# A gate row applied to the finished projection on VectorE instead of to eight weight tiles on GpSimd

## The chip, the cores and the metric

The kernel runs on one core of one Trainium2 chip. The metric is the device time of one execution in microseconds (us), the median of several runs. The engines are named as in the profile: PE is TensorE, with its weight loads listed apart as PEld; DVE is VectorE; ACT is ScalarE; POOL is GpSimd; SP is SyncE, which here only issues transfers.

## The reference, cut to what matters

Two transformer blocks run on 256 tokens of width 1024. The change lies in the second block, where its mixer ends:

```python
sh1, sc1, gt1, sh2, sc2, gt2 = jnp.split(mod, N_MOD, axis=-1)
...
merged = jax.nn.sigmoid(gate_sb) * br_sb + jax.nn.sigmoid(gate_d) * br_d
x = x + gt1[:, None, :] * (merged @ w_out[layer])

h2 = modulate(rms_norm(x, g_ffn[layer]), sh2, sc2)
x = x + gt2[:, None, :] * peer_ffn(h2, w_pq[layer], peer_keys[layer], peer_u[layer], peer_v[layer])
```

`gt1` is one row of 1024 numbers. It scales the columns of the product, so it may be multiplied into the columns of `w_out` before the product, or into the product after it.

## The kernel before, in words

Everything is computed in float32. A product with a weight is made of three matmuls: a weight tile of 128 rows by 1024 columns is split into a high half `whi` (a rounded copy, made by ACT at L228) and a low half `wlo` (the tile minus its high half, a subtraction at L233, mostly on DVE, for a few tiles on POOL), and the activations likewise. Each weight tile is loaded whole (512 KB) into one of four buffers `raw`, in a ring: a load is issued by SP at L201 as soon as the low half of the tile four places ahead has been taken. `specs` lists the tiles in the order of use, with flags: "G" (multiply by the gate row first), "L" (keep the halves in the pool `late`, which has 7 buffers here), "P" (low half on POOL). `_split` handles one tile of that list: it issues the loads that have come due, and then splits the tile.

The stretch that the change touches comes in this order:

- The merge: for eight column tiles n, PE multiplies two attention outputs (`sbT`, `dT`) with the branch weights (L274: 12 matmuls and 6 of 256 columns for each n, so 18), DVE multiplies the two results with sigmoid gates (L1308, L1309, which read PSUM) and adds them (L1310), ACT copies the high half into `mT` (L1311), and DVE takes the low half (L1312).
- The projection with `w_out` of the second block, whose eight tiles are called out0 to out7 below: 12 matmuls of 512 columns for each tile. The first four tiles are done between the merges (`formA_acc`, L860), the last four in `acc_tail` (L875), which first finishes both halves of token tile 0 (24 matmuls), then the left and then the right half of token tile 1 (12 each). The results stand in four PSUM banks `acc`.
- The end (`epi`), for each token tile: add `acc` to the residual `x` (`add_x`, L1008), sums of squares on ACT (`sumsq`, L313), a reciprocal root in some ten small DVE instructions (`rsqrt`, L295 to L306), scaling (`scale_x`, L358 on ACT and L359 on DVE, giving `xn`), transposes on PE (L369), then scale and shift and the split into `h_hi` and `h_lo` (`norm_Tt`, L380 to L384).
- The next product, with `w_pq` (L1103, the first four of its 16 tiles called pq0 to pq3; their low halves are taken on POOL), then 12 more tiles at L274, the scores, a top-16 search on DVE, and two passes over 128 tiles each of `peer_u` (L1597) and `peer_v` (L1682). Beside these, rows for the first 96 tokens are gathered by POOL's queue into `ug`.

A scheduler sets the order of the instructions on each engine when the kernel is built, from its own estimate of times. Each engine works through its own list strictly in order, so an instruction that waits holds up all that stand behind it on that engine. Here are the functions that the change touches:

Of the kernel before, what the change touches and what calls it, by code (L numbers as in the profile page):

```python
# [9 lines left out]
F32 = mybir.dt.float32  # L10
# [6 lines left out]
OP = mybir.AluOpType  # L17
# [115 lines left out]
class Kernel:  # L133
# [4 lines left out]
    def specs(self):  # L138
        io = self.io
        sp = []  # L140

        def add(w, idx, flag="", late=0):
            idx = list(idx)
            for n, i in enumerate(idx):
                sp.append((w[i], flag + ("L" if n >= len(idx) - late else "")))
        add(io["w_in"], (0, 1, 2, 3, 12, 13, 14, 15, 4, 8, 5, 9, 6, 10, 7, 11))
        add(io["w_glu"], range(2), "R")
        add(io["w_out"], range(8), late=4)
        add(io["w_gu"], range(8), late=self.GL)
        nv = 0  # L150
        for j in range(4, NF):
            add(io["w_gu"], (2 * j, 2 * j + 1))
            add(io["w_down"], (j - 4,))
            for _ in range(self.JV[j]):
                add(io["w_in2"], (8 + nv,), "L")
                nv += 1
            if j >= NF - 4:
                add(io["w_down"], (j,), "L")
        add(io["w_in2"], range(8 + nv, 12))
        add(io["w_in2"], list(range(8)) + list(range(12, 46)))  # L160
        add(io["w_br"], range(6))
        for i in range(8):
            add(io["w_out2"], (i,), "G" + ("L" if i > 3 else ""))
        for i in range(4):
            add(io["w_pq"], (i,), "LP")
        add(io["w_pq"], range(4, 16))
        self.nwide = len(sp)
        add(io["peer_u"], range(128), "R")
        add(io["peer_v"], range(128), "R")
        return sp  # L170
# [39 lines left out]
    def _split(self, pin=lambda i: i):  # L210
        j = self.nsplit
        while self.ndma < len(self.wspec):
            early = self.depth > self.RAW and self.ndma - self.nwide < 24 + 2 * self.RB
            if self.ndma >= j + self.depth + (4 if early else 0):
                break
            self._dma()
        t = self.rawt.pop(j)
        flag = self.wspec[j][1]
        if "R" in flag:
            self.wt[j] = t  # L220
            self.nsplit += 1
            return
        if "G" in flag:
            self.nc.gpsimd.tensor_tensor(t, t, self.gt1, OP.mult)  # L224
        late = "L" in flag
        hi = (self.late if late else self.his).tile([128, 1024], F32R, name="whi")
        lo = (self.late if late else self.los).tile([128, 1024], F32R, name="wlo")
        i = self.nc.scalar.activation(hi, t, AF.Copy)  # L228
        pin(i)
        if self.fenced:  # L230
            self.behind(i, self.fence[0])
        e = self.nc.gpsimd if j in self.POOL_LO or "P" in flag else self.nc.vector
        i = e.tensor_tensor(lo, t, hi.bitcast(F32), OP.subtract)  # L233
        pin(i)
        if self.fenced:
            self.fenced -= 1
            if e is self.nc.vector:
                self.behind(i, self.fence[1])
        self.wt[j] = (hi, lo)
        self.nsplit += 1  # L240
# [761 lines left out]
                self.norm_Tt(H, xn, self.cols[:, C_GFFN:], None, self.h2[0], self.h2[1], tt)  # L1002
            self.acc_tail(acc, [(self.mixT, k) for k in range(4, 8)], False, epi, pre=self.PRE[0])

    def add_x(self, acc, tt, pin):
        for n in range(2):
            x = self.x[:, tt, 512 * n:512 * n + 512]
            i = self.nc.vector.tensor_tensor(x, x, acc[2 * tt + n], OP.add)  # L1008
            if tt and n < pin:
                self.tc.keep_in_program_order(i)  # L1010

# [210 lines left out]
    def block2(self):  # L1222
        nc, V, A, tc = self.nc, self.nc.vector, self.nc.scalar, self.tc
        with ExitStack() as st:
# [67 lines left out]
            with tc.tile_pool(name="mrg", bufs=2) as M, self.ps_pool("pa") as pa:  # L1292
                mT = [M.tile([128, 8, 256], F32R, name=f"mT{i}", bufs=1) for i in range(2)]
                acc = [self.bank(pa, f"acc{i}") for i in range(4)]
                for half in range(2):
                    wb = self.wget(2)
                    wa = [self.wget(1), self.wget(0)]
                    for q in range(4):
                        n = 4 * half + q
                        ps = self.psum()  # L1300
                        va = lambda w: (lambda k: w[:, (q % 2) * 512 + k * 128:(q % 2) * 512 + k * 128 + 128])
                        vb = lambda w: (lambda k: w[:, q * 256 + k * 128:q * 256 + k * 128 + 128])
                        self.mm3(ps[:, 0:256], va(wa[q // 2][0]), va(wa[q // 2][1]), lambda k: self.sbT[0][:, k],
                                 lambda k: self.sbT[1][:, k], 4)
                        self.mm3(ps[:, 256:512], vb(wb[0]), vb(wb[1]), lambda k: self.dT[0][:, k],
                                 lambda k: self.dT[1][:, k], 2)
                        a, b = [M.tile([128, 256], F32, name=f"mg{i}") for i in "ab"]
                        V.tensor_tensor(a, ps[:, 0:256], gates[:, n], OP.mult)  # L1308
                        V.tensor_tensor(b, ps[:, 256:512], gates[:, 8 + n], OP.mult)  # L1309
                        V.tensor_tensor(a, a, b, OP.add)  # L1310
                        A.activation(mT[0][:, n], a, AF.Copy)  # L1311
                        V.tensor_tensor(mT[1][:, n], a, mT[0][:, n].bitcast(F32), OP.subtract)  # L1312
                for n in range(4):
                    self.formA_acc(acc, mT, n, n == 0, False)
                self.h4 = self.bigT("h4")
                g, sh = self.mod_col(M, 4, "G2"), self.mod_col(M, 3, "sh2")

                def epi(tt):
                    self.add_x(acc, tt, self.XP[2])
                    yield  # L1320
                    r = self.rstd(M, self.x, tt, "n4")
                    if tt == 0:
                        self.r4 = self.cols[:, C_NCOL:C_NCOL + 1]
                        V.tensor_copy(self.r4, r)
                    xn = self.scale_x(M, self.x, r, tt)
                    yield
                    self.norm_Tt(M, xn, g, sh, self.h4[0], self.h4[1], tt)
                self.acc_tail(acc, [(mT, k) for k in range(4, 8)], False, epi, pre=self.PRE[2])


# [437 lines left out]
```

## Time and profile before

| what | value |
|---|---|
| median of 3 runs | 1325.82 us (1325.56 to 1333.4) |
| the profiled execution's own time | 1333.33 us |
| its span, first to last instruction | 1331.6 us |
| PE busy | 1246.1 us (94%) |
| DVE busy | 925.5 us (70%) |
| POOL busy | 464.3 us (35%) |
| POOL, L224, `raw` times `gt1` | 8 instructions, 21.2 us |

The busy shares are means over the whole span and hide that its stages have different limits. The rows further down come from one stretch of some 50 us, and each shows in square brackets how long the engine stood idle before the instruction, and what ended that wait. Two successive instructions of one engine overlap a little in these listings, so the distance from one start to the next is the better measure of what one costs in a sequence.

### The profile page before, as it was taken

What the parts mean: (1) busy time and instruction counts of PE and PEld (TensorE: products, weight loads), DVE (VectorE), ACT (ScalarE), POOL (GpSimd) and SP (SyncE); (2) the same over time, 40 slices, a digit from 0 to 9 for tenths busy, and PEclk for the clock granted to TensorE, in tenths of its full rate; (3) what the DMA queues carried; (4) which work ended last, traced back from release to release, by engine and by line L of the source; (5) the groups of instructions that cost most, each with busy time, mean ns of one, the idle gap of its engine ahead of it and who ended that gap; (6) DMA issues with size and microseconds to landing.
All of it is one profiled execution on the core that took longest, in us unless ns stands there. A gap on an engine that the chain in (4) does not pass through costs nothing.

```text
span 1331.6 us, 22565 instructions
## 1 busy us (share of the span) xinstructions
PE 1246.1 (94%) x8649; PEld 1162.7 (87%) x8650; DVE 925.5 (70%) x1806; ACT 447.2 (34%) x895; POOL 464.3 (35%) x408
## 2 busy tenths in 40 slices
PE   6798989999999999988899999999999999999994
PEld 5687869988979898986699999999999999888884
DVE  8995765899668887459789957677764444444455
ACT  5336655666556745634542212212110000000001
POOL 5931021555104745026300432222233333333331
PEclk9997889999999998998899999999999999999996
DMA  6322445989726645434758899999999999999993
GB/s 201 97 94 64 131 163 207 316 303 332 245 84 231 210 139 189 131 124 165 252 199 297 302 409 376 364 355 353 366 364 408 409 409 408 408 409 408 409 407 121
DMA packets 103116, 361.50 MB, mean 271 GB/s; under 512 B 15136, under 2 KB 15328, under 8 KB 102624
## 3 DMA queue, kind: packets, MB, share of 16 engines
q1 hardware_dynamic: 71904, 251.28, 51.9%
q0 software_dynamic: 30816, 108.26, 21.4%
q8 instruction: 68, 1.11, 0.3%
q10 hardware_dynamic: 288, 0.52, 0.1%
q14 instruction: 40, 0.33, 0.1%
HBM read 356.22 MB, written 2.12 MB: 269 GB/s over the span
## 4 chain that ended last, share of the span: by engine, by line
PE 44%; DMA 20%; DVE 18%; issue 9%; POOL 6%; ACT 2%; ACTq 0%; POOLq 0%; SPq 0%; DVEq 0%
PE m L1597 17%; DMA ug<-peer_v,slot 15%; PE m L274 14%; DVE wlo L233 4%; PE acc L860 3%; PE acc L1103 3%; DVE sacc L1518 2%; POOL ug L1501 2%; DMA adaw<-w_ada 2%; PE g L1553 1%; POOL adaacc L412 1%; PE acc L875 1%; PE pq L1103 1%; POOL adaacc L414 1%; DMA bias<-bias 1%
## 5 line engine op out<-in xcount | busy, mean ns | idle before, releaser
L1682 PE MATMUL acc<-act,raw 128*128 128x160 f32 x2048 | 296.4, 303 | 8.7 <-DMA raw<-peer_v 2.0
L1682 PEld LDWEIGHTS acc<-act,raw 128*128 128x128 f32 x2048 | 280.1, 190 | 24.9 <-DMA raw<-peer_v 23.3
L1597 PE MATMUL m<-hN,raw 128*128 128x160 f32 x2048 | 283.4, 300 | 2.6 <-ACT act L1607 2.6
L233 DVE TENSOR_TENSOR wlo<-raw,whi 128x1024 fp32r<-128x1024 f32 x150 | 237.7, 1595 | 67.4 <-ACT whi L228 64.7
L1597 PEld LDWEIGHTS m<-hN,raw 128*128 128x128 f32 x2048 | 278.9, 190 | 2.8 <-ACT act L1607 2.8
L228 ACT ACTIVATE whi<-raw 128x1024 fp32r<-128x1024 f32 x166 | 174.0, 1055 | 138.9 <-PE m L274 56.0
L1518 DVE SCALAR_TENSOR_TENSOR sacc<-ug,sw,sacc 128x1024 f32<-128x1024 f32 x94 | 120.8, 1285 | 122.2 <-DMA ug<-peer_v,slot 122.1
L1501 POOL DMA_INDIRECT ug<-u_rows,slot x96 | 97.5, 1015 | 212.8 <-DVE ug L1506 131.2
L1506 DVE SCALAR_TENSOR_TENSOR ug<-ug,hrow 128x1024 f32<-128x1024 f32 x96 | 117.2, 1222 | 45.8 <-DMA ug<-u_rows,slot 45.7
L1501 POOL DMA_INDIRECT ug<-peer_v,slot x96 | 91.5, 953 | 159.1 <-DVE sacc L1518 144.8
L274 PE MATMUL m<-h_hi,wlo 128*128 128x256 f32 x768 | 113.4, 288 | 7.4 <-DVE wlo L233 5.0
L274 PE MATMUL m<-h_hi,whi 128*128 128x256 f32 x768 | 117.1, 292 | 2.6 <-ACT h_hi L918 2.6
L274 PE MATMUL m<-h_lo,whi 128*128 128x256 f32 x768 | 117.0, 291 | 2.0 <-DVE h_lo L919 2.0
L274 PEld LDWEIGHTS m<-h_hi,whi 128*128 128x128 f32 x768 | 105.8, 197 | 7.1 <-ACT h_hi L918 3.5
L274 PEld LDWEIGHTS m<-h_hi,wlo 128*128 128x128 f32 x768 | 101.6, 193 | 9.8 <-DVE wlo L233 6.0
L274 PEld LDWEIGHTS m<-h_lo,whi 128*128 128x128 f32 x768 | 105.0, 197 | 3.3 <-DVE h_lo L919 2.4
L1689 ACT ACTIVATE fT<-acc,gt 128x160 f32<-128x160 f32 x4 | 1.3, 393 | 247.0 <-DVE fT L1691 247.0
L412 POOL TENSOR_TENSOR adaacc<-adaacc,adaw 128x1024 f32<-128x1024 f32 x24 | 66.5, 2770 | 49.3 <-ACT adaw L411 48.8
L1615 ACT ACTIVATE ut<-m 128x8 f32<-128x8 f32 (+19 forms) x84 | 20.2, 241 | 130.6 <-PE m L1597 130.5
L1618 DVE TENSOR_TENSOR act<-act,ut 128x8 f32<-128x8 f32 (+19 forms) x84 | 20.8, 247 | 52.2 <-ACT ut L1615 52.1
L233 POOL TENSOR_TENSOR wlo<-raw,whi 128x1024 fp32r<-128x1024 f32 x16 | 40.4, 2534 | 27.4 <-ACT whi L228 22.9
L224 POOL TENSOR_TENSOR raw<-raw,gt 128x1024 f32<-128x1024 f32 x8 | 21.2, 2664 | 56.9 <-DVE wlo L233 42.4
(522 smaller groups left out, 1774.4 us busy)
## 6 DMA issues: line engine op xcount, KB each, us to landing
raw<-peer_u SPq DMA_DIRECT2D x128, 512.0 KB, 6.6
raw<-peer_v SPq DMA_DIRECT2D x128, 512.0 KB, 20.1
raw<-w_in SPq DMA_DIRECT2D x62, 512.0 KB, 4.3
adaw<-w_ada SPq DMA_DIRECT2D x48, 512.0 KB, 5.3
raw<-w_gu SPq DMA_DIRECT2D x44, 512.0 KB, 4.9
raw<-w_down SPq DMA_DIRECT2D x22, 512.0 KB, 4.6
raw<-w_out SPq DMA_DIRECT2D x16, 512.0 KB, 3.4
raw<-w_pq SPq DMA_DIRECT2D x16, 512.0 KB, 5.0
```

Source lines behind the costliest of these rows:

```text
L224: self.nc.gpsimd.tensor_tensor(t, t, self.gt1, OP.mult)
L228: i = self.nc.scalar.activation(hi, t, AF.Copy)
L233: i = e.tensor_tensor(lo, t, hi.bitcast(F32), OP.subtract)
L274: self.nc.tensor.matmul(out, w(k), x(k), start=start and c == 0, stop=stop and c == last)
L412: G.tensor_tensor(accs[1], accs[1], w, OP.add)
L860: self.nc.tensor.matmul(acc[2 * tt + n], a[:, k, tt * 128:tt * 128 + 128], w[:, 512 * n:512 * n + 512], start=first and (tt, n) not in see ...
L1103: self.nc.tensor.matmul(out, a[:, 2 * c + kk, tt * 128:tt * 128 + 128], w[:, 512 * kk:512 * kk + 512], start=c + i + kk == 0, stop=c == 3 ...
L1501: G.indirect_dma_start(t, None, rows, bass.IndirectOffsetOnAxis(self.slot[:, 0, s:s + 1].bitcast(U32), 0))
L1506: V.scalar_tensor_tensor(t, t, 1.0, self.hrow[g], op0=OP.mult, op1=OP.mult, accum_out=self.sdot[:, s:s + 1])
L1518: self.last = V.scalar_tensor_tensor(self.sacc[g], t, w, self.sacc[g], op0=OP.mult, op1=OP.add)
L1597: m = nc.tensor.matmul(ps, w[:, 128 * k:128 * k + 128], hN[:, k], start=k == 0, stop=k == 7)
L1682: nc.tensor.matmul(part(d), w[:, 128 * d:128 * d + 128], at(i), start=i == 0 and d % 2 == 0, stop=i == 127, skip_group_check=True)
```

## The change

The multiplication by `gt1` at L224 goes, with the flag "G" that called for it. In `add_x` the product `acc` is first multiplied by the gate row into a new tile `gx` (one buffer of 128x512), and `gx` is then added to `x`. Only the second block's mixer passes a gate; the other two calls of `add_x` stay as they were.

```diff
         for i in range(8):
-            add(io["w_out2"], (i,), "G" + ("L" if i > 3 else ""))
+            add(io["w_out2"], (i,), "L" if i > 3 else "")
...
-        if "G" in flag:
-            self.nc.gpsimd.tensor_tensor(t, t, self.gt1, OP.mult)
...
-    def add_x(self, acc, tt, pin):
+    def add_x(self, acc, tt, pin, gate=None):
         for n in range(2):
             x = self.x[:, tt, 512 * n:512 * n + 512]
-            i = self.nc.vector.tensor_tensor(x, x, acc[2 * tt + n], OP.add)
+            y = acc[2 * tt + n]
+            if gate is not None:
+                y = gate[0].tile([128, 512], F32, name="gx", bufs=1)
+                self.nc.vector.tensor_tensor(y, acc[2 * tt + n], gate[1][:, 512 * n:512 * n + 512], OP.mult)
+            i = self.nc.vector.tensor_tensor(x, x, y, OP.add)
...
-                    self.add_x(acc, tt, self.XP[2])
+                    self.add_x(acc, tt, self.XP[2], (M, self.gt1))
```

The lists of all engines are the same up to this stretch. In it, the line numbers of the changed kernel are smaller by 2 between L224 and the addition, and larger by 2 behind it. POOL's list from the merge to the end of the stretch, before:

```order
L224 TENSOR_TENSOR raw<-raw,gt_5364 128x1024
L458 DMA G_6430<-modd 128x8x1
L458 DMA sh_6432<-modd 128x8x1
L224 TENSOR_TENSOR raw<-raw,gt_5364 128x1024 x7
L1470 DMA ug<-modd 96x1024 x2
L233 TENSOR_TENSOR wlo<-raw,whi 128x1024 x4
L1479 DMA hrow_6767<-ug 64x1024 x2
```

and after:

```order
L456 DMA G_6424<-modd 128x8x1
L456 DMA sh_6426<-modd 128x8x1
L231 TENSOR_TENSOR wlo<-raw,whi 128x1024 x4
L1472 DMA ug<-modd 96x1024 x2
L382 TENSOR_TENSOR h_lo<-hT,h_hi 128x128 x2
L1481 DMA hrow_6767<-ug 64x1024 x2
```

The eight multiplications are gone, the four low halves of pq0 to pq3 come ahead of the transfers into `ug`, and two `h_lo` now come ahead of those into `hrow`.

ACT's list at the last merges, where raw_6345 and raw_6344 are out4, raw_6228 and raw_6338 are out2 and out3, and mga_6279 to mga_6331 belong to n = 5 to 7; before:

```order
L1311 ACTIVATE mT0_6100<-mga_6279 128x256
L228 ACTIVATE whi_6355<-raw_6228 128x1024
L228 ACTIVATE whi_6374<-raw_6338 128x1024
L1311 ACTIVATE mT0_6100<-mga_6305 128x256
L228 ACTIVATE whi_6393<-raw_6345 128x1024
L1311 ACTIVATE mT0_6100<-mga_6331 128x256
L228 ACTIVATE whi_6412<-raw_6352 128x1024
```

and after:

```order
L226 ACTIVATE whi_6388<-raw_6344 128x1024
L1313 ACTIVATE mT0_6100<-mga_6279 128x256
L226 ACTIVATE whi_6352<-raw_6228 128x1024
L226 ACTIVATE whi_6370<-raw_6338 128x1024
L1313 ACTIVATE mT0_6100<-mga_6305 128x256
L226 ACTIVATE whi_6406<-raw_6350 128x1024
L226 ACTIVATE whi_6430<-raw_6368 128x1024
L226 ACTIVATE whi_6436<-raw_6386 128x1024
L1313 ACTIVATE mT0_6100<-mga_6331 128x256
```

The split of out4 has moved ahead of the copy for n = 5 and of the splits of out2 and out3, and the splits of out5 to out7 stand ahead of the copy for n = 7.

DVE's list at the end, where acc0 and acc1 belong to token tile 0, acc2 and acc3 to token tile 1, and n4_r0 and n4_r1 are their reciprocal roots; before, from the first addition to the third:

```order
L1008 TENSOR_TENSOR x_78<-x_78,acc0_6102 128x512
L1008 TENSOR_TENSOR x_78<-x_78,acc1_6103 128x512
...
L301 SCALAR_TENSOR_TENSOR rs_t_6530<-n4_r0_6528,rs_a_6532 128x1
...
L359 TENSOR_SCALAR xn0_6545<-x_78,n4_r0_6528 128x512
L1008 TENSOR_TENSOR x_78<-x_78,acc2_6104 128x512
```

and after:

```order
L1009 TENSOR_TENSOR gx_6512<-acc0_6102,gt1_5364 128x512
L1010 TENSOR_TENSOR x_78<-x_78,gx_6512 128x512
L1009 TENSOR_TENSOR gx_6515<-acc1_6103,gt1_5364 128x512
...
L1010 TENSOR_TENSOR x_78<-x_78,gx_6515 128x512
L1009 TENSOR_TENSOR gx_6544<-acc2_6104,gt1_5364 128x512
...
L1010 TENSOR_TENSOR x_78<-x_78,gx_6544 128x512
...
L1009 TENSOR_TENSOR gx_6547<-acc3_6105,gt1_5364 128x512
...
L1010 TENSOR_TENSOR x_78<-x_78,gx_6547 128x512
...
L357 TENSOR_SCALAR xn0_6541<-x_78,n4_r0_6524 128x512
```

All four multiplications and additions, those of token tile 1 too, now stand ahead of the scaling of token tile 0.

## Rows read from the trace of the kernel before

**Rows 1.** Stretches: start:end, length; busy time (instructions) of PE, PEld, DVE, ACT, POOL; clock, DMA share, GB/s.
```profile
616.00:629.00 13.00, 8.83 (x29) 6.40 (x28) 11.96 (x9) 4.78 (x5) 9.41 (x5) 0.74 0.63 213
...
749.00:987.00 238.00, 237.65 (x1928) 236.89 (x1929) 167.73 (x351) 45.78 (x204) 71.00 (x68) 1.00 0.98 370
```

**Rows 2.** POOL in order of time: start, length, engine, line, instruction, count, wait.
```profile
584.21 2.37 POOL L224 TENSOR_TENSOR raw<-raw,gt 128x1024 f32<-128x1024 f32 x1 [42.40 <-DVE wlo L233]
...
613.14 8.67 POOL L224 TENSOR_TENSOR raw<-raw,gt 128x1024 f32<-128x1024 f32 x3 [4.46 <-ACT mT L1311]
...
629.60 7.06 POOL L233 TENSOR_TENSOR wlo<-raw,whi 128x1024 fp32r<-128x1024 f32 x3 [3.00 <-ACT whi L228]
```

**Rows 3.** DVE in order of time, in the merge and the projection.
```profile
585.05 0.69 DVE L324 TENSOR_TENSOR dT<-tr,dT 128x512 fp32r<-128x512 f32 x1 [1.06 <-ACT dT L323]
...
597.99 3.04 DVE L233 TENSOR_TENSOR wlo<-raw,whi 128x1024 fp32r<-128x1024 f32 x1 [0.78 <-PE m L274]
...
611.03 1.21 DVE L233 TENSOR_TENSOR wlo<-raw,whi 128x1024 fp32r<-128x1024 f32 x1
612.16 0.41 DVE L1310 TENSOR_TENSOR mga<-mga,mgb 128x256 f32<-128x256 f32 x1
...
613.63 2.62 DVE L1312 TENSOR_TENSOR mT<-mga,mT 128x256 fp32r<-128x256 f32 x1
```

**Rows 4.** DVE's groups, 585 to 629 us: busy us, mean ns, idle before.
```profile
L233 DVE TENSOR_TENSOR wlo<-raw,whi 128x1024 fp32r<-128x1024 f32 x10 | 19.5, 1956 | 0.8 <-PE m L274 0.8
...
L1310 DVE TENSOR_TENSOR mga<-mga,mgb 128x256 f32<-128x256 f32 x8 | 8.2, 1034 | 0.0
...
L1312 DVE TENSOR_TENSOR mT<-mga,mT 128x256 fp32r<-128x256 f32 x8 | 7.7, 964 | 0.5 <-ACT mT L1311 0.3
```

**Rows 5.** PE's waits from 585 to 642 us: total, times, longest.
```profile
PE acc L875 <- DVE wlo L233: 4.2, 2, 2.2
...
PE m L274 <- ACT whi L228: 2.7, 1, 2.7
```

**Rows 6.** PE in order of time.
```profile
588.92 0.64 PE L274 MATMUL m<-dT,whi 128*128 128x256 f32 x4
589.40 0.40 PE L274 MATMUL m<-dT,wlo 128*128 128x256 f32 x2
...
628.76 0.63 PE L875 MATMUL acc<-whi,mT 128*128 128x512 f32 x2
...
634.13 0.40 PE L875 MATMUL acc<-wlo,mT 128*128 128x512 f32 x1
638.16 1.97 PE L369 MATMUL m<-eye,xn 128*128 128x128 f32 x8 [3.63 <-DVE xn L359]
641.55 1.48 PE L1103 MATMUL pq<-whi,h_hi 128*128 128x512 f32 x2 [1.43 <-ACT h_hi L383]
```

**Rows 7.** SP's issue of the load of out4; then loads by tensor, us to landing.
```profile
601.10 0.33 SPq L201 DMA_DIRECT2D raw<-w_out  x1
...
raw<-w_pq SPq DMA_DIRECT2D x11, 512.0 KB, 5.3
raw<-w_out SPq DMA_DIRECT2D x8, 512.0 KB, 3.9
```

**Rows 8.** DVE in the end of the mixer; the last row is ACT's.
```profile
628.73 1.29 DVE L1008 TENSOR_TENSOR x<-x,acc 128x512 f32<-128x512 f32 x2 [1.04 <-PE acc L875]
...
632.05 2.33 DVE L297 SCALAR_TENSOR_TENSOR rs_a<-n_ss,rs_a 128x1 f32<-128x1 f32 x1 [0.46 <-ACT sqj L313]
...
634.80 1.88 DVE L301 SCALAR_TENSOR_TENSOR rs_t<-n_r,rs_a 128x1 f32<-128x1 f32 x1
...
640.41 0.40 DVE L382 TENSOR_SCALAR hT<-m,G,sh 128x128 f32<-128x128 f32 x1
...
643.55 0.22 DVE L301 SCALAR_TENSOR_TENSOR rs_t<-n_r,rs_a 128x1 f32<-128x1 f32 x1
...
630.70 0.62 ACT L313 ACTIVATE sqj<-x 128x512 f32<-128x512 f32 x1
```

## The prediction

> **What bounds the kernel now.** First read the stretches [rows 1]. From 749 to 987 us PE is busy for 237.65 of 238, and the transfers fill 0.98 of their engines. The stretch of the change looks different: from 616 to 629 PE is busy for 8.83 of 13 us at a granted clock of 0.74, while DVE is busy for 11.96 of those 13, which looks like a full engine.
>
> Next read why DVE is full, by laying POOL's list [rows 2] beside DVE's [rows 3]. On DVE an instruction of 128x256 with both inputs in SBUF takes 0.41 us at 612.16, where POOL computes nothing, but 2.62 at 613.63, beside the gate multiplications that POOL began at 613.14. A low half L233 takes 1.21 at 611.03 and 3.04 at 597.99, beside another of the eight. So a DVE instruction with two inputs in SBUF that meets a GpSimd multiplication stands still until that ends, and then does its own work. L324 at 585.05, which reads one of its inputs from PSUM, took 0.69 in the middle of the gate of 584.21 to 586.58: that form is not held. The groups [rows 4] give the sum: ten L233 took 19.5 in place of 10 x 1.21, eight L1310 8.2 and eight L1312 7.7 in place of 8 x 0.41 each; 7.4 + 4.9 + 4.4 = 16.7 us of standing still. One of the ten stood behind a low half of w_pq on POOL and not behind a gate, which leaves some 15.
>
> Last read what PE waits for [rows 5]: 4.2 us for two low halves from DVE, and 2.7 for one high half, for which ACT was late because the copy ahead of it waited for a DVE addition. So DVE, held by POOL, sets the pace of PE here.
>
> **The change, part by part.** *Removed: eight gate multiplications, and with them some 15 us of DVE.* What this is worth is set by what is late next, and that is PE itself. Take PE from the last row without a wait, at 589.40 [rows 6]. Four matmuls of 256 columns went from 588.92 to 589.40, 0.12 each, so the two of that row are through at 589.64. Four merges are left, 4 x 18 = 72 matmuls of 256 columns, and the projection, 8 x 12 = 96 of 512. The last 24 of these start between 628.76 and 634.13, 23 steps of 0.2335. At those rates and without a wait it takes 72 x 0.12 + 96 x 0.2335 = 31.1 us. The last matmul then starts at 620.5 in place of 634.13, 13.7 us earlier; 6.9 of that are the two waits above, the rest smaller waits and the slow clock after them.
>
> Do the operands keep up? I walked the changed lists with the undisturbed lengths. Two L1310 end at 588.6; a copy to mT (0.42) and a split (1.05) on ACT follow, so PE goes on at 589.85, 0.2 late. Out0's low half needs a buffer that PE frees, now at 593.4, and ends at 595.0. That frees a raw buffer for out4: before, the same end, at 597.99 + 3.04, released the issue at 601.10 [rows 7]. With 3.9 us to landing out4 is there at 598.9, and its halves are done at 600.0 and 601.8. Out2's high half comes at 602.2 and is wanted at 604.0; out7 is loaded from 604.5, its halves are done by 610.7, and it is wanted at 613.6. The smallest reserve is 1.8 us, so PE stays busy. This term: **-13.5 us**, with both halves of token tile 0 done at 614.8.
>
> *Added and moved: the end.* Before, it took 12.8 us from the first addition at 628.73 to the first product with w_pq at 641.55 [rows 6, 8]. What differs:
> (a) Two multiplications for token tile 0, 0.65 each like the additions (1.29 for two): +1.3. The gate row is in SBUF already, so no transfer is added.
> (b) The four instructions of token tile 1 now stand ahead of xn0: 4 x 0.65 = +2.6.
> (c) Before, L297 and L301 took 2.33 and 1.88 beside POOL's low halves of w_pq from 629.60. Undisturbed they take about 0.2, as L301 does at 643.55: -3.8.
> (d) These four POOL instructions of 2.35 us (7.06 for three) stay. By the loads they run from 611 to 618.9 (pq0 to pq2), and from 621.4 to 623.8 for pq3, whose buffer is free only when out4 is used up, and whose split stands behind two sums of squares on ACT. The second new addition meets pq2 (+1.5) and L301 meets pq3 (+2.2): +3.7.
> (e) ACT's sum of squares began at 630.70 without a wait shown, behind splits of w_pq, though x was ready at 629.4: -1.3.
> (f) hT came at 640.41, 2.25 after the transposes at 638.16, because two additions and the row for ug stood ahead; four transposes need 1.0 of that (1.97 for eight): -1.2.
> Sum: **+1.3**. Besides, the transposes of token tile 1 now stand behind only three products, and their xn1 is some 0.5 late by the walk: **+0.5**.
>
> On (d) a rule speaks against the change. The Trainium skill, "SBUF — State Buffer", section "Who interferes with whom", says that a DVE instruction with two SBUF inputs contends with a GpSimd instruction that reads SBUF, and that one with a single SBUF input does not. The old addition read acc from PSUM; the new one reads x and gx, both in SBUF. The row at 613.63 agrees for the same form with smaller tiles. If the new addition passed as L324 did, the sum would be 1.5 better, 1312.6.
>
> *Passed on.* What follows is driven by this end: PE goes on with hardly a gap up to 987, and the loads behind it go out as buffers come free. I pass the shift on whole.
>
> Sum: -13.5 + 1.3 + 0.5 = -11.7 us. The profiled execution would take 1333.3 - 11.7 = 1321.6. Of the four executions shown two took 1325.6 and 1325.8, two 1333.3 and 1333.4; nothing in the change bears on that difference, so against the median of 1325.8 the forecast is **1314.1**.
>
> Bounds of the unknown part: (d) can cost nothing, if the low halves of w_pq fall into gaps, which gives -15.4 or 1310.4, or more than I took, as in rival 1.
>
> **The rivals.**
> 1. *The end loses more to the four POOL subtractions.* Loads of w_pq took 5.3 us at the median [rows 7]. If pq2 lands 3 to 4 us later than I took, its split on ACT holds the first sum of squares by 2.4, and its low half then meets another small instruction of the root (+2.2). That gives -7.1: 1318.7. For it: ACT's list still has three splits of w_pq ahead of that sum. Against it: the transfers into ug, which went beside these loads before, now come behind them.
> 2. *No collision at all*: 1310.4, as above. For it: a shift of 2 us in either list is enough. Against it: four instructions of 2.35 us in a stretch of 14.
> 3. *The shift does not arrive.* From 749 the transfers are busy for 0.98 of the time. If they ran by a clock of their own, the end would stay: 1326. Against it: they wait for buffers that PE or DVE frees, and PE has no gap from 749 to 987.
> 4. *Slower: ACT's list.* The split of out4 now stands ahead of the copy for n = 5, and those of out5 to out7 ahead of the copy for n = 7. So all of DVE behind them waits for two landings one after the other, out4's and out7's. The walk has 0.7 us to spare at the first and 2.9 at the second. With L us to landing the cost is 2 x (L - 3.9) - 3.6: nothing up to 5.7, the whole gain at 11.6, and 2.9 us more than the gain at 13, which is 1328.7. The medians here are 3.9 and 5.3 [rows 7], far from that.
>
> That the change does not do what it says can be left out: POOL's changed list holds no L224.
>
> **How the numbers follow.** Forecast 0.62; rival 1 0.16; rival 2 0.13; rival 3 0.05; rival 4 0.04. A measurement of this kernel can tell about 1% (13 us) from no change, so the forecast itself lies within 1%. Faster by over 1% means below 1312.6: rival 2 and the near edge of the forecast, 0.25. Slower by over 1% needs rival 4 at its worst: 0.02. The rest, 0.73, is within 1%. The range goes from 1309 (rival 2 and 1.4 of error in the walk) to 1321 (rival 1 and 2.3 of error); rivals 3 and 4 are left out.
>
> **What would show it.** Right: from 585 on PE has no wait of over 1 us until its last product with w_out, which starts near 620; L1310, L1312 and L233 on DVE take 0.41, 0.42 and 1.22 throughout; the clock of the stretch is 1.00; the first product with w_pq starts near 629; loads of w_out land in about 4 us. Step (d) shows as one or two instructions of over 1.5 us among the new additions and L301. Wrong: waits of PE for halves of out4 to out7 (rival 4), a first product with w_pq later than 632 (rival 1), or a gap of PE between 657 and 987 that was not there before.

## The result, and the profile after

The changed kernel takes 1315.14 us (median of 6 runs, 1311.89 to 1318.84), the kernel before 1328.09 beside it (6 runs, 1325.56 to 1333.4): a ratio of 0.9906, interval 0.9881 to 0.993. The forecast was 1314.1, a gain of 11.7 on a kernel before of 1325.8; the gain is 12.95 on one of 1328.1.

The six executions of each kernel differ by 7 to 8 us among themselves. The profiled execution of after took 1311.89 us, with a span of 1309.8, 21.8 less than that of before. Of these, 9.0 lie ahead of the change, where all lists are equal: the copy to dT, with which the last merges begin, stands at 585.05 in before [rows 3] and at 576.04 in after. So all traces are compared from that copy on; below, "dT" is its start.

In the list of DVE of after, this copy and then, for token tile 0, the first multiplication, the two additions, the step L299 of the root (L301 in before) and the scaling:

```profile
576.04 0.69 DVE L322 TENSOR_TENSOR dT<-tr,dT 128x512 fp32r<-128x512 f32 x1 [1.05 <-ACT dT L321]
...
605.99 0.69 DVE L1009 TENSOR_TENSOR gx<-acc,gt 128x512 f32<-128x512 f32 x1 [3.85 <-PE acc L873]
606.72 0.69 DVE L1010 TENSOR_TENSOR x<-x,gx 128x512 f32<-128x512 f32 x1
...
608.27 1.96 DVE L1010 TENSOR_TENSOR x<-x,gx 128x512 f32<-128x512 f32 x1
...
612.07 2.30 DVE L299 SCALAR_TENSOR_TENSOR rs_t<-n_r,rs_a 128x1 f32<-128x1 f32 x1
...
616.74 0.48 DVE L357 TENSOR_SCALAR xn<-x,n_r 128x512 f32<-128x512 f32 x1
```

In the groups of DVE's instructions from 576 to 603 us of after (count, busy time, mean ns, idle time ahead), the rows that answer to [rows 4]:

```profile
L231 DVE TENSOR_TENSOR wlo<-raw,whi 128x1024 fp32r<-128x1024 f32 x10 | 12.1, 1219 | 1.5 <-ACT whi L226 1.3 <-PE acc L858 0.2
...
L1314 DVE TENSOR_TENSOR mT<-mga,mT 128x256 fp32r<-128x256 f32 x8 | 3.4, 419 | 0.3 <-ACT mT L1313 0.2
...
L1312 DVE TENSOR_TENSOR mga<-mga,mgb 128x256 f32<-128x256 f32 x8 | 3.3, 418 | 0.0
```

Ten low halves take 12.1 in place of 19.5 us, and the two kinds of 128x256 take 3.3 and 3.4 in place of 8.2 and 7.7: nothing stands still. Of PE's waits from 576 to 632, which answers to the stretch of [rows 5], two are left: 0.7 us for dT, which before has too, and this one, at the end:

```profile
PE m L367 <- DVE xn L357: 5.5, 1, 5.5
```

PE itself, from the row that answers to 589.40 [rows 6], over the last product with w_out and the transposes of xn0, to the first product with w_pq:

```profile
580.39 0.40 PE L272 MATMUL m<-dT,wlo 128*128 128x256 f32 x2
...
611.39 0.40 PE L873 MATMUL acc<-wlo,mT 128*128 128x512 f32 x1
617.27 1.97 PE L367 MATMUL m<-eye,xn 128*128 128x128 f32 x8 [5.48 <-DVE xn L357]
619.23 1.48 PE L1105 MATMUL pq<-whi,h_hi 128*128 128x512 f32 x2
```

From 580.39 to 611.39 it is 31.00 us, before 44.73: 13.73 less, all of the gain and a little more. The granted clock is 1.00 throughout. The end, from the first addition to the first product with w_pq, took 12.82 us [rows 6, 8] and takes 13.24, from the first multiplication. POOL's low halves of pq0 to pq3 say where it lost:

```profile
601.96 7.73 POOL L231 TENSOR_TENSOR wlo<-raw,whi 128x1024 fp32r<-128x1024 f32 x3 [24.19 <-ACT whi L226]
612.01 2.34 POOL L231 TENSOR_TENSOR wlo<-raw,whi 128x1024 fp32r<-128x1024 f32 x1 [2.33 <-ACT whi L226]
```

The addition of 608.27 waits for the end of pq2's low half, at 609.69, and then does its own work (1.27 lost); L299 ends with pq3's (2.08 lost). The addition of 606.72, of the same form, lost nothing. It began 0.04 us ahead of pq2's low half, which waited for it instead: POOL's third instruction took 2.92 us, the two ahead of it 2.45 and 2.41.

### The profile page after: what moved, and what is told of

It reads as the page before. It is cut to its first block, busy times and chain, and to the rows that moved or that the text cites. A ratio compares the mean times of both kernels' runs of the same rounds, so it can differ in the third digit from the quotient of the medians.

```text
span 1309.8 us, 22554 instructions
## 1 busy us (share of the span) xinstructions
PE 1238.3 (95%) x8649; PEld 1158.9 (88%) x8650; DVE 909.0 (69%) x1810; ACT 447.7 (34%) x895; POOL 445.3 (34%) x400
## 3 DMA queue, kind: packets, MB, share of 16 engines
q0 software_dynamic: 30816, 108.26, 21.8%
## 4 chain that ended last, share of the span: by engine, by line
PE 52%; DMA 19%; DVE 15%; issue 6%; POOL 5%; ACT 3%; SPq 0%; DVEq 0%; POOLq 0%; ACTq 0%
PE m L1599 17%; PE m L272 16%; DMA ug<-peer_v,slot 16%; PE acc L858 4%; DVE wlo L231 3%; PE acc L1105 2%; DVE sacc L1520 2%; POOL ug L1503 2%; DMA adaw<-w_ada 2%; PE acc L873 1%; PE g L1555 1%; PE pq L1105 1%; DVE adaacc L407 1%; POOL adaacc L412 1%; DVE work L1337 1%
## 5 line engine op out<-in xcount | busy, mean ns | idle before, releaser
L231 DVE TENSOR_TENSOR wlo<-raw,whi 128x1024 fp32r<-128x1024 f32 x150 | 229.3, 1539 | 69.7 <-ACT whi L226 68.2
L1609 ACT ACTIVATE act<-m 128x160 f32<-128x160 f32 x44 | 13.1, 304 | 69.6 <-PE m L1599 67.7
```

## The experiments

The theory (A): a DVE instruction with both inputs in SBUF stands still while POOL reads SBUF, and this held DVE, and PE behind it, for 13.7 us in before; the end costs little. The rivals for the long stretch are the longer way of a tile from its landing over the gate to the split (B, and D where the gate is on DVE) and POOL's being busy whatever it does (C); a further one is that the work moved to the end costs far more than it seems (E). The letters count anew for the experiments on the end, from psum_gate on. All columns but the last are in us from dT. The first column less 4.35 is PE's stretch, the 44.73 and 31.00 us above; "routing" is the first product behind those with the first four tiles of w_pq.

| kernel | last w_out product | first w_pq product | routing | end of the span | routing to end |
|---|---|---|---|---|---|
| before | 49.08 | 56.50 | 72.06 | 746.55 | 674.49 |
| after | 35.35 | 43.19 | 57.95 | 733.76 | 675.81 |
| dead_gate | 46.34 | 53.26 | 68.73 | 744.18 | 675.45 |
| dead_memset | 35.36 | 44.17 | 59.32 | 732.80 | 673.48 |
| gate_on_dve | 46.04 | 50.57 | 66.64 | 739.64 | 673.00 |
| dve_all | 44.38 | 49.06 | 65.61 | 738.63 | 673.02 |
| no_gate | 35.36 | 43.47 | 59.04 | 732.42 | 673.38 |
| psum_gate | 35.37 | 41.03 | 57.91 | 732.73 | 674.82 |
| tt1_behind | 35.35 | 42.54 | 60.68 | 735.68 | 675.00 |
| psum_and_behind | 35.36 | 40.59 | 58.07 | 733.69 | 675.62 |
| fill_pause | 35.36 | 44.80 | 59.50 | 735.97 | 676.47 |
| fill_psum | 35.37 | 41.46 | 56.25 | 731.60 | 675.35 |

The last column varies from 673.0 to 676.5 in no order that fits the edits. This scatter bounds what a comparison of whole spans can tell.

**dead_gate.** The changed kernel, and POOL multiplies 960 of the 1024 columns of each w_out tile by the gate once more, into a tile `scr` that nothing reads. The allocation of `scr` is left out here.

```
+            add(io["w_out2"], (i,), "D" + ("L" if i > 3 else ""))
...
+        if "D" in flag:
+            for c in (0, 544):
+                self.nc.gpsimd.tensor_tensor(self.scr, t[:, c:c + 480], self.gt1[:, c:c + 480], OP.mult)
```

> The changed kernel, and GpSimd multiplies each of the eight w_out tiles by the gate row as before, but into a scratch tile that nobody reads (two instructions of 480 columns for each tile). Nothing waits for these products. Measured in the trace: the stretch from the last merge of the first half (start of the last two matmuls of n = 3) to the start of the last w_out matmul, 44.7 us before and 31.0 after. Theory A (a GpSimd multiplication holds every DVE instruction with two inputs in SBUF that meets it): the stretch goes back to 39 to 46 us, L1310, L1312 and L233 on DVE show stretched instructions again, and the time to 1321 to 1329 us. Rival B (the change paid because a gate product no longer stood between a tile's landing and its split, so each turn of the ring of buffers got 2.4 us shorter): nothing waits for the dead products, so the stretch stays at 31 to 33 us and the time at that of the changed kernel, 1314 to 1317 us.

Measured: 1323.43 us, ratio to before 0.9977 (0.9949 to 1.0005). PE's stretch is 42.0 us. DVE's groups from 583 to 620:

```profile
L234 DVE TENSOR_TENSOR wlo<-raw,whi 128x1024 fp32r<-128x1024 f32 x10 | 14.8, 1491 | 0.0
L1316 DVE TENSOR_TENSOR mga<-mga,mgb 128x256 f32<-128x256 f32 x8 | 9.1, 1153 | 0.0
L1318 DVE TENSOR_TENSOR mT<-mga,mT 128x256 fp32r<-128x256 f32 x8 | 8.2, 1031 | 0.0
L1314 DVE TENSOR_TENSOR mga<-m,gates 128x256 f32<-128x256 f32 x8 | 3.3, 415 | 0.9 <-PE m L275 0.8
```

And PE waits for DVE again:

```profile
PE acc L876 <- DVE mT L1318: 3.4, 1, 3.4
```

No split waits for these multiplications, so the way from landing to split is no longer than in after; only one load, of w_pq at 621.31, waited 0.9 us for one of them. They alone bring back 11 of the 13.7 us. The other 2.7 may be the longer way, or the other lengths of these instructions; nothing here separates the two. The eight of L1314, which read m in PSUM, keep 0.415.

**dead_memset.** At the same place one column of each tile is read, and POOL then writes `scr` three times without reading.

```
+        if "D" in flag:
+            self.nc.gpsimd.tensor_tensor(self.scr[:, 0:1], t[:, 0:1], self.gt1[:, 0:1], OP.mult)
+            for _ in range(3):
+                self.nc.gpsimd.memset(self.scr, 0.0)
```

> As the kernel with dead products, but GpSimd only reads one column of each tile (to wait for its landing) and then fills the scratch tile with zeros three times (480 columns each), so it is about as busy but writes only. Theory A in its narrow form (what collides is the reading of SBUF, as the Trainium skill, SBUF - State Buffer, Who interferes with whom, has it): the stretch stays at 31 to 33 us and the time at that of the changed kernel. Rival C (any GpSimd instruction holds DVE, reading or writing): the stretch goes to 36 to 44 us and the time up by 5 to 12 us over the changed kernel.

Measured: 1314.68 us, ratio 0.9918 (0.9888 to 0.9948), stretch 31.0. POOL's and DVE's groups from 574 to 600:

```profile
L226 POOL MEMSET scr<- 128x480 f32 x24 | 12.0, 500 | 1.3
```
```profile
L235 DVE TENSOR_TENSOR wlo<-raw,whi 128x1024 fp32r<-128x1024 f32 x10 | 12.1, 1219 | 1.4 <-ACT whi L230 1.3 <-PE acc L862 0.2
```

POOL is less busy than with the dead products (some 14 us against 23), but its writing overlaps 16 of the 26 DVE instructions with two inputs in SBUF, and none is longer for it: the low halves keep their 1219 ns. So it is POOL's reading that holds DVE, not its being busy; rival C falls. The Trainium skill, "SBUF — State Buffer", section "Who interferes with whom", says just this, that a DVE instruction with two inputs in SBUF contends with a GpSimd instruction that reads SBUF and not with one that only writes; the traces of dead_gate (1491 ns) and dead_memset (1219) agree.

**gate_on_dve.** The kernel before, with the multiplication of the weight tiles on DVE.

```
-            self.nc.gpsimd.tensor_tensor(t, t, self.gt1, OP.mult)
+            self.nc.vector.tensor_tensor(t, t, self.gt1, OP.mult)
```

> The kernel before, with the eight gate multiplications of the weight tiles on DVE in place of GpSimd. They add 8 x 1.2 = 9.7 us to a DVE that looked full. Theory A: of DVE's time in the stretch some 15 us were standing still, so it can take them: 22.5 us of own work and 9.7 more are 32 us, about what PE needs. The stretch is 33 to 38 us, against 44.7 before, and the time 7 to 12 us below the kernel before. Rival D (DVE was full of work of its own, and the change paid by taking a wait from its neighbours): the stretch grows to 48 us or more, and the kernel is slower than before.

Measured: 1323.02 us, ratio 0.9976 (0.9949 to 1.0004), stretch 41.7: between the two expectations, so neither number held. DVE was not full of work of its own, since it took the multiplications and the stretch still became 3 us shorter. DVE, POOL and PE at the end of the stretch:

```profile
614.46 2.93 DVE L233 TENSOR_TENSOR wlo<-raw,whi 128x1024 fp32r<-128x1024 f32 x1
617.31 2.56 DVE L1312 TENSOR_TENSOR mT<-mga,mT 128x256 fp32r<-128x256 f32 x1
```
```profile
613.91 5.67 POOL L233 TENSOR_TENSOR wlo<-raw,whi 128x1024 fp32r<-128x1024 f32 x2
```
```profile
619.92 1.22 PE L875 MATMUL acc<-whi,mT 128*128 128x512 f32 x2 [2.97 <-DVE mT L1312]
```

With DVE as the late engine its last instructions slid beside POOL's low halves of pq0 and pq1, which add 1.7 and 2.1. That this is the cause, dve_all tests.

**dve_all.** The kernel of gate_on_dve, with the low halves of the first four w_pq tiles on DVE too.

```
-            add(io["w_pq"], (i,), "LP")
+            add(io["w_pq"], (i,), "L")
```

> The kernel before with the gate on DVE, and with the low halves of the first four w_pq tiles on DVE as well, so that GpSimd computes nothing in the stretch. In the run with the gate on DVE PE's stretch took 41.7 us, and two of its last DVE instructions took 2.93 and 2.56 beside low halves of w_pq on GpSimd. Theory A: these two cost 3.8, and the two low halves that now stand ahead of the last copy to mT give 2.3 of that back: 40.1 us (39.5 to 40.8). Rival D (the chain from landing over gate and split sets it, not GpSimd): 41.5 or more.

Measured in one run: 1324.14 us; stretch 40.0, as theory A gave. What keeps it from 31.0 is DVE's own work: seven multiplications and two low halves more are 11 us, and from 590 to 620 DVE (the third busy time) is busy for 29.28 of 30, PE (the first) for 25.38.

```profile
590.00:620.00 30.00, 25.38 (x140) 20.93 (x140) 29.28 (x45) 13.25 (x18) 1.06 (x2) 1.00 0.58 182
```

**no_gate.** The changed kernel without any gate; its output leaves the gate gt1 out.

```
-                    self.add_x(acc, tt, self.XP[2], (M, self.gt1))
+                    self.add_x(acc, tt, self.XP[2])
```

> The changed kernel without any gate: neither the weight tiles nor the product is multiplied by the gate row, so that part of the computation is left out. It shows what the moved work costs at the end of the mixer. From the first addition (or multiplication) to the first product with w_pq it took 12.8 us before and 13.2 after. By the terms of the prediction (four DVE instructions of 0.65 us less on the path, the second token tile behind the first again, but additions in front of hT and some collisions with the low halves of w_pq left): 9 to 12 us, the stretch of PE unchanged at 31.0, the time 1 to 4 us below the changed kernel. Rival E (the moved multiplications cost much and the gain would be far larger without them): 7 us or less, and 6 us or more below the changed kernel.

Measured: 1312.92 us, ratio 0.99 (0.9858 to 0.9941). The end is 13.51 us, longer than with the gate: a miss for both. Two steps of the root meet the low halves:

```profile
611.35 1.53 DVE L295 SCALAR_TENSOR_TENSOR rs_a<-n_ss,rs_a 128x1 f32<-128x1 f32 x1 [0.46 <-ACT sqj L311]
...
613.29 1.89 DVE L299 SCALAR_TENSOR_TENSOR rs_t<-n_r,rs_a 128x1 f32<-128x1 f32 x1
```

Besides, ACT's first sum of squares stands behind two splits again: it begins at 610.00, 2.8 us after x is ready. So without the gate other waits fill the end, and it is no shorter. The order of the lists has changed with the edit, so what the multiplications would cost in one and the same order isn't shown.

**psum_gate.** The changed kernel, with the gate multiplied in place in PSUM, so that the addition reads one input there.

```
-                y = gate[0].tile([128, 512], F32, name="gx", bufs=1)
-                self.nc.vector.tensor_tensor(y, acc[2 * tt + n], gate[1][:, 512 * n:512 * n + 512], OP.mult)
+                self.nc.vector.tensor_tensor(y, y, gate[1][:, 512 * n:512 * n + 512], OP.mult)
```

> The changed kernel, but the gate multiplies the projection in place in PSUM, so that the addition to x reads one input from PSUM again. Theory A (a DVE instruction meets a GpSimd subtraction only if both its inputs are in SBUF): the second addition, which took 1.96 us beside a low half of w_pq, takes 0.69; the two reductions for the pairs now stand behind xn0 (-0.5); the small step L299 is still held, since the low half that holds it comes earlier by as much. From the first multiplication to xn0 8.9 us in place of 10.75, to the first product with w_pq 11.4 (10.9 to 11.9) in place of 13.24; if L299 slips out as well, 2 less. Rival B (it is held by its place beside GpSimd, wherever its inputs lie): 12.5 to 13.3. In time -1.8 us by A, about 1313, which the clock on the whole kernel hardly tells from 1315.

Measured: 1312.19 us, ratio 0.9904 (0.9872 to 0.9936). From the first multiplication at 609.14 it is 9.02 us to xn0 and 11.06 to the first product with w_pq, as theory A gave. DVE and POOL:

```profile
610.35 1.28 DVE L1010 TENSOR_TENSOR x<-x,acc 128x512 f32<-128x512 f32 x2
...
613.88 2.33 DVE L299 SCALAR_TENSOR_TENSOR rs_t<-n_r,rs_a 128x1 f32<-128x1 f32 x1
```
```profile
605.15 7.20 POOL L231 TENSOR_TENSOR wlo<-raw,whi 128x1024 fp32r<-128x1024 f32 x3 [24.27 <-ACT whi L226]
613.82 2.37 POOL L231 TENSOR_TENSOR wlo<-raw,whi 128x1024 fp32r<-128x1024 f32 x1 [1.47 <-ACT whi L226]
```

Two additions take 1.28 in the middle of POOL's three. But the first product with w_pq, 2.2 us earlier than in after, brings nothing: routing begins at 57.91 and 57.95. The reason is in the stretches of two us (length; busy PE, PEld, DVE, ACT, POOL; granted clock, DMA share, GB/s), first of after:

```profile
614.00:616.00 2.00, 0.00 (x0) 0.00 (x0) 2.00 (x8) 0.00 (x0) 0.83 (x2) 0.53 0.00 0
616.00:618.00 2.00, 0.73 (x4) 0.73 (x5) 1.88 (x12) 1.35 (x3) 0.60 (x2) 0.50 0.60 135
618.00:620.00 2.00, 2.00 (x8) 1.21 (x6) 1.50 (x8) 1.10 (x4) 0.00 (x0) 0.50 0.98 360
620.00:622.00 2.00, 2.00 (x10) 1.61 (x10) 1.72 (x7) 1.94 (x7) 0.00 (x0) 0.77 0.99 371
622.00:624.00 2.00, 2.00 (x13) 1.64 (x12) 1.62 (x4) 1.83 (x6) 0.99 (x2) 1.00 0.97 301
```

and of psum_gate:

```profile
618.00:620.00 2.00, 1.12 (x8) 0.86 (x8) 1.93 (x11) 1.16 (x4) 0.82 (x2) 0.91 0.95 229
620.00:622.00 2.00, 1.80 (x4) 1.21 (x5) 1.96 (x12) 1.83 (x6) 0.00 (x0) 0.50 0.86 307
622.00:624.00 2.00, 2.00 (x7) 1.51 (x6) 1.48 (x5) 1.83 (x7) 0.46 (x1) 0.50 1.00 414
624.00:626.00 2.00, 2.00 (x10) 1.90 (x9) 1.32 (x3) 1.18 (x5) 0.46 (x1) 0.50 0.36 135
626.00:628.00 2.00, 2.00 (x9) 1.60 (x9) 2.00 (x5) 1.19 (x4) 0.00 (x0) 0.89 0.00 0
```

In after PE stands from 611.8 to 617.27; the clock falls to 1.2 GHz in this wait and is back at 2.4 GHz at 620.9, so of the products with w_pq (from 619.23) 1.7 us go at 1.2 GHz. In psum_gate PE stands from 614.9 to 618.69, goes on at 2.4 GHz, and the clock is low from 619.6 to 626.5, from the end of the first transposes on: the first 6.3 us of work from the first product with w_pq (620.20), the transposes of token tile 1 among it, go at 1.2 GHz. (The expectation for fill_psum below, 5.9, was short by 0.4.) Half of 6.3 less half of 1.7 is 2.3 us, about the 2.2 that were won.

**tt1_behind.** The changed kernel, with the multiplications of token tile 1 kept in the order of the program.

```
-                self.nc.vector.tensor_tensor(y, acc[2 * tt + n], gate[1][:, 512 * n:512 * n + 512], OP.mult)
+                (self.tc.keep_in_program_order if tt and n < pin else id)(self.nc.vector.tensor_tensor(y, acc[2 * tt + n], gate[1][:, 512 * n:512 * n + 512], OP.mult))
```

> The changed kernel, with the multiplications of token tile 1 kept in the order of the program, so that its four instructions stand behind xn0 as its two did in the kernel before. The prediction priced these four ahead of xn0 at 2.6 us. Theory A: two of the four are covered, one by the second sum of squares on ACT and one by the time at which the last low half on GpSimd ends, which L299 waits for in any case; from the first multiplication to xn0 9.3 us in place of 10.75, to the first product with w_pq 11.8 (11.4 to 12.3) in place of 13.24. Rival B (all four are on the path): 10.6 or less. Rival C (none is): 13.2.

Measured: 1315.87 us, ratio 0.9937 (0.9912 to 0.9962); xn0 after 9.71 us, the first product after 12.59, between A and C. The first addition took 2.75 here, 0.8 more than the second in after; less that, it is A's 11.8. The first was held this time because pq2's low half began ahead of it, 0.2 us; in after it was the other way round, by 0.04. And L299 is no longer held, but a later step is, up to the end of pq3's low half again:

```profile
606.50 2.75 DVE L1010 TENSOR_TENSOR x<-x,gx 128x512 f32<-128x512 f32 x1
...
612.60 2.33 DVE L302 SCALAR_TENSOR_TENSOR n_r<-rs_t,rs_h 128x1 f32<-128x1 f32 x1
```

The 0.65 us won at the first product are more than lost by routing, which begins 2.7 later than in after: 5.4 us of the products with w_pq go at 1.2 GHz in place of 1.7 (half of the difference, 1.8, is lost), and PE waits for 0.9 more; the remaining 0.7 weren't traced.

**psum_and_behind.** Both edits in one.

```
-                y = gate[0].tile([128, 512], F32, name="gx", bufs=1)
-                self.nc.vector.tensor_tensor(y, acc[2 * tt + n], gate[1][:, 512 * n:512 * n + 512], OP.mult)
+                i = self.nc.vector.tensor_tensor(y, y, gate[1][:, 512 * n:512 * n + 512], OP.mult)
+                _ = self.tc.keep_in_program_order(i) if tt and n < pin else None
```

> Both edits in one: the gate in place in PSUM, and token tile 1 behind xn0. By theory A the chain holds two multiplications, two additions, one sum of squares and the steps of the root, about 5 us to xn0 if no step of the root meets the low half of pq3, and about 7.5 if one does; to the first product with w_pq 7.6 to 10.2 us in place of 13.24, so 1309.5 to 1312 us in all. Rival: the root waits for the end of the low half of pq3 whatever stands ahead of it, and that end hardly moves: 10.5 or more.

Measured: 1312.68 us, ratio 0.9898 (0.9868 to 0.9927). From the first multiplication to xn0 7.2 us, as expected for a step that meets pq3 (now L304); to the first product 10.6, outside A's range and what the rival gave. The rest is lost not at the root but at hT: three instructions of token tile 1 stand between xn0 and it, and PE waits for it.

```profile
615.53 2.31 DVE L304 SCALAR_TENSOR_TENSOR n_r<-rs_t,n_r 128x1 f32<-128x1 f32 x1
```
```profile
621.40 0.77 PE L1105 MATMUL pq<-whi,h_hi 128*128 128x512 f32 x1 [1.52 <-ACT hT L378]
```

**fill_pause** and **fill_psum.** The changed kernel and psum_gate, with products that nothing reads in PE's wait for xn0 (40 and 26). What passes the number `fill` on is left out here.

```
+        ps = self.psum() if fill else None
+        for _ in range(fill):
+            r = items[0][0][0][:, items[0][1]]
+            self.tc.keep_in_program_order(self.nc.tensor.matmul(ps[:, 0:256], r[:, 0:128], r, start=True, stop=True))
```

> The changed kernel, with 40 products of 256 columns on PE behind the last product with w_out, whose result nothing reads: they fill some 4.8 of the 5.5 us in which PE waits for xn0. In the changed kernel the granted clock fell in this wait to 1.2 GHz, and PE's first 3.6 us after it (617.3 to 620.9) went at that clock. Theory A (the clock falls since PE stands still): it stays at 2.4 GHz, these 3.6 us take 1.8, and from dT to the first product of the routing stage it is 56.1 us in place of 57.95. Rival B (the clock falls in this stage whatever PE does): the low stretch of 6.8 us lies on work alone, 59 or more. Rival C (what sets the stage is not PE): 57.9.

> The version with the gate in place in PSUM, with 26 such products in PE's wait of 3.75 us. There the first product with w_pq came 2.1 us earlier than in the changed kernel and the routing stage at the same time, since 5.9 us of work went at 1.2 GHz behind the wait. Theory A: these take 2.9 us less, dT to the first product of the routing stage 55.0 us in place of 57.9, and the whole 3 us less than the changed kernel, 0.9885 of the kernel before. Rival B: 57.9 or more.

Measured: fill_pause 1315.26 us, ratio 0.9932 (0.99 to 0.9964), routing at 59.50, not 56.1. It doesn't tell the theories apart: its first addition, held by pq2's low half, took 2.60 us, hT came to stand behind the scaling of token tile 1, and PE still had two waits of over 1 us, behind which the clock fell (0.51 from 622 to 624).

fill_psum is clean: 1309.16 us, ratio 0.988 (0.9841 to 0.9918). The filler ends at 615.6, the clock is 1.00 in every stretch from 612 to 626, two of them here, and routing begins at 56.25, 1.66 earlier than in psum_gate.

```profile
612.30 3.26 PE L881 MATMUL m<-mT 128*128 128x256 f32 x26
616.25 1.10 PE L367 MATMUL m<-eye,xn 128*128 128x128 f32 x8 [0.69 <-DVE xn L357]
618.16 0.49 PE L1109 MATMUL pq<-whi,h_hi 128*128 128x512 f32 x1 [0.81 <-ACT h_hi L381]
```
```profile
618.00:620.00 2.00, 1.64 (x8) 1.07 (x9) 1.86 (x9) 1.94 (x7) 0.00 (x0) 1.00 0.97 377
620.00:622.00 2.00, 2.00 (x13) 1.64 (x12) 1.45 (x7) 1.82 (x6) 0.46 (x1) 1.00 0.91 373
```

Of the 2.9 expected 1.3 are missing: the first product comes 0.4 later, since PE waits for a half of h (0.81), and the rest is lost between the products and wasn't traced. Rival B, that the clock falls whatever PE does, falls. The version has the lowest median and the shortest span from dT of all, 2.2 us less than after; on whole times it beats the kernel before, and isn't told apart from the changed one.

## Why the prediction was right, point by point

- **PE's stretch, -13.7 less 0.2.** 13.73 measured, and no wait in it. dead_gate and dead_memset show the reason, for 11 of them: the multiplications' reading of SBUF, not the longer way to the split. For the other 2.7 this stays open.
- **Do the operands keep up.** They do; rival 4's waits for out4 and out7 don't show.
- **(a) +1.3.** From the first multiplication to the second addition, undisturbed, 608.27 + 0.69 - 605.99 = 2.97, against 1.29 for two additions [rows 8]: +1.7. One buffer for gx and a step of the root between them make the difference.
- **(b) +2.6.** Too much. One of the four runs beside ACT's second sum of squares, and an addition lies in the time up to the end of pq3's low half; tt1_behind puts the whole, up to xn0, at 1.0, or 1.8 with its worse collision taken out.
- **(c) -3.8 and (d) +3.7.** Both as said. The new addition lost 1.27 (forecast 1.5), L299 2.08 (2.2). psum_gate shows that the addition is held for its second input in SBUF. That the second addition met pq2 and not the first was luck: in dead_memset, with the same end, the first began 0.01 us behind pq2's low half, took 2.94 and lost 2.3, and the end took 14.21. Which step of the root meets pq3 differs too, L299, L302 or L304 in three kernels, but one did in each changed kernel.
- **(e) -1.3 and (f) -1.2.** The first sum of squares begins at 607.44, with x ready at 607.41; hT stands right behind the transposes, which begin 1.96 ahead of the first product in place of 3.39: -1.4.
- **The end in all:** +0.42 where +1.3 was forecast, mostly by (b). **Transposes of token tile 1, +0.5:** 0, PE has no wait there.
- **What the sum lacked:** the clock. From the first product with w_pq to routing before took 15.56 us and after 14.76, 0.8 less: the same products, of which 3.5 us go at 1.2 GHz in before and 1.7 in after, where more of the slow time lies in PE's wait ahead of them.
- **Passed on whole.** From routing to the end 674.49 and 675.81, inside what the twelve traces scatter. Rival 3 falls.

The four parts, -13.73 + 0.42 - 0.80 + 1.32, make the 12.79 by which the spans from dT differ; the medians differ by 12.95. So the mechanism and its one large term were right, and the closeness of the sum is partly luck: up to routing the forecast was 2.4 us short, all its errors on one side, and the 1.32 behind routing, which lies within the scatter, hid half of that. Rival 1 (1318.7) and rival 2 (1310.4) priced the end higher and lower, and neither came: both collisions are there, and none is worse than said. Whole times alone would hardly tell them from the forecast; the trace does.

## What to carry to other kernels

When DVE is full, look at how long its instructions take beside POOL's and alone: a second engine that takes work off DVE and reads SBUF for it can cost DVE more than the work (here some 15 us, where the eight multiplications on DVE itself are 8 x 1.22). Choose the form of an added instruction by where its inputs lie; with one input in PSUM the addition of this kernel was free of a wait that cost 1.3 to 2.1 us in three others. And a shorter wait of PE isn't yet a gain: look at the granted clock behind it before you count it.

## What the runs showed of the hardware that was not expected

In psum_gate PE's wait was 3.75 us in place of 5.5, the clock fell only after PE had gone on, and the time at 1.2 GHz lay on the work behind the wait (6.3 us of it, 1.7 in after). The wait's length alone doesn't settle this: in tt1_behind it was 4.45 us, the clock fell within it, and 5.4 us of products were slow all the same. What sets the moment isn't shown. The Trainium skill, "TensorE: Matmul & The Clock Gate", section "HAM oscillation — how this bites in real kernels", tells of work that starts at the low clock behind a wait; after agrees (its first products behind the wait go at 0.50), and psum_gate adds that the clock can fall later. When 26 products that nothing reads filled the wait, the clock stayed at 2.4 GHz.

In the collisions traced here the one that comes second waits for the other's end, so the two sides pay very differently. Three low halves on POOL, 7.06 us in before [rows 2], took 7.73 in after, longer by about the 0.69 of the addition that was ahead of the third; a step of the root of 0.22 us that came second took up to 2.38. A few hundredths of a us decided between the two: the same addition cost POOL 0.5 us in after and DVE 2.3 in dead_memset.
